# A decoder layer with expert lookup: where the first output projection keeps its tiles, and how a half-filled tile is picked

## The chip, the cores and the metric

The kernel runs on one core of a Trainium2 chip. A core has five engines that each work through a queue of their own in order: TensorE (PE, with its weight loads as PEld), VectorE (DVE), ScalarE (ACT), GpSimd (POOL) and SyncE (SP, which here only starts transfers). They wait for each other by semaphores. The metric is the device time of one execution in microseconds; a time is the median of several runs.

## The reference

One layer of a decoder over 1024 prompt tokens and 8 short sequences of 8 tokens (64 rows): two token mixers beside each other, an output projection, an expert mixer, and an embedding with a gate.

```python
def layer(h, p_l, pos, s_ret, s_wkv, s_shift, lp):
    xn = rmsnorm(h, norm_mix)
    proj = xn @ w_in
    ...                                   # retention in chunks of 128; RWKV-7 scan
    h = h + jnp.concatenate([o_ret, o_rw], axis=-1) @ w_out
    h = h + peer(rmsnorm(h, norm_ffn), peer_wq, peer_keys, peer_u, peer_v)
    gate = jax.nn.sigmoid((rmsnorm(h, ple_norm) @ ple_gate).astype(jnp.float32))
    h = h + (gate * (p_l @ ple_proj)).astype(h.dtype)

def peer(xn, wq, keys, u_tab, v_tab):     # per token, 8 heads, 2 half keys of 128
    q = (xb @ wq).reshape(PEER_BLOCK, PEER_HEADS, 2, PEER_DKEY // 2)
    s = jnp.einsum('phcd,hcnd->phcn', q, keys).astype(jnp.float32)
    sv, si = lax.top_k(s, PEER_TOPK)                        # 16 best of 128, for 16 (h, c)
    cand = sv[:, :, 0, :, None] + sv[:, :, 1, None, :]
    cv, ci = lax.top_k(cand.reshape(...), PEER_TOPK)        # 16 best pairs of each head
    e = ...                                                 # 128 expert numbers a token
    gsm = jax.nn.softmax(cv, axis=-1)
    hval = jnp.einsum('pd,phkd->phk', xb, u_tab[e])
    act = jax.nn.gelu(hval) * gsm
    return jnp.einsum('phk,phkd->pd', act, v_tab[e])
```

All matrices are float32; the output is all rows after a last norm, and the mixers' states.

## The kernel before

The 1088 rows are nine tiles of rows: tiles 0 to 7 hold 128 prompt tokens each, tile 8 the 64 sample rows. The work goes in stages.

*Input projections.* `group_a` runs three times, over tiles 0 and 1 (A0), 2 and 3 (A1), 4 to 8 (A2). It normalises and transposes the rows (`norm_T`, PSUM tile `ntr`), multiplies by `w_ret` (`a_ret`, PSUM tile `pret`, weights `wraw`, `wh`, `wl`) and by `w_rw` (`a_rw`, `prw`). Each float32 product is three matmuls of rounded halves (`mm3`, lines 336, 337 and 339). PSUM tiles come from banks with a tag: `a` has two buffers, `b` three, `d` one. A2 takes `pret` and `prw` from `b`; its `ntr` came from `a`.

*First tile.* While A1 runs, tile 0 goes through the mixers (`first_mix`, up to the tile `tail`) and then through the output projection, `c_rows`: transposes (`etr`), sixteen matmuls with blocks `cw` of `w_out` (`ewo`, line 625), the residual `ch`, the norm with rows `cgr`, and the store of the normalised row to memory (`xd`). `c_rows` took its tiles from a pool `co0` with a ring of six for blocks of 2 KB a partition. That pool lay behind A1's pools and was closed with them.

*Early experts.* `early` loads tile 0's row again (`exn`, line 1215), computes its query (`epq`), its top-k, and then its experts one by one: `gather` fetches for the j-th expert of 128 tokens a row of `u` each (an indirect DMA from POOL, `grow`, line 1161), which VectorE multiplies with the token (line 1175); then the same with `v` and a sum (line 1189). Tile 1 follows. Tiles 8, 2 and 3 are gathered in the same way later; tile 8 has its 64 rows laid twice, so that 128 partitions hold half of a token's experts each.

*Mixers.* `group_b` takes the other eight tiles through both mixers and `c_rows` (in a pool `co`, ring of four), with early's gathers in between.

*Query.* `c_query` goes over 16 pairs of head and half key: weights, `pq` for two groups of tiles, the scores `psc` for each tile, and for each tile a `pick` of five VectorE operations (16 best of 128). `topk` then combines them and makes the expert numbers (`eq`, `ef`). For tile 8 its numbers were copied by DMAs to the second half of the partitions.

*Dense experts.* Tiles 4 to 7 use all experts with a mask: `hidden`, `gates`, `dense_fused`, `dense_stored` (`ph`, `py`, `yT`), while the gathers of tiles 8, 2 and 3 go on beside them. `ple` ends the layer, tile by tile, tile 3 last: it adds tile 3's sum `gacc` (line 1447).

What decides the order on each engine: the code is written as generators that are stepped in turn (`interleave`, `behind`); a scheduler at build time then orders each engine's instructions by priority and its own estimate of durations. Pools stand on one stack on the right side of SBUF, and a tile that takes over the memory of a closed pool waits for the last use of what lay there.

## Time and profile before

| | us |
|---|---|
| median of 3 runs | 3610.72 (3601.78 to 3620.93) |
| profiled execution, its own time | 3621.93 |
| its span | 3620.2 |
| end of A1 on TensorE | about 262 |
| first `pret` of A2 | 307.73 |
| end of A2's projections on TensorE | about 573 |
| mixers end, last `hns` of `pY` | 1579.5 |
| query stage, first and last score matmul | 1637.3, 1809.5 |
| dense stage, first and last sum into `yT` | 2456.1, 3451.7 |

The profiled execution took 11 us more than the median, so sums are made against its own time and carried to the median afterwards. Rows of the timeline read: start, length, engine (with q: its queue of transfers and waits), line, operation, what it writes and reads, count, and in brackets the idle time before it and what ended that. The rows with two ends and many columns are stretches of the span.

### The profile page before, as it was taken

What the parts mean: (1) busy time and instruction counts of PE and PEld (TensorE: products, weight loads), DVE (VectorE), ACT (ScalarE), POOL (GpSimd) and SP (SyncE); (2) the same over time, 40 slices, a digit from 0 to 9 for tenths busy, and PEclk for the clock granted to TensorE, in tenths of its full rate; (3) what the DMA queues carried; (4) which work ended last, traced back from release to release, by engine and by line L of the source; (5) the groups of instructions that cost most, each with busy time, mean ns of one, the idle gap of its engine ahead of it and who ended that gap; (6) DMA issues with size and microseconds to landing.
All of it is one profiled execution on the core that took longest, in us unless ns stands there. A gap on an engine that the chain in (4) does not pass through costs nothing. (4 is left out here: it accounts for less than half of the span.)

```text
span 3620.2 us, 51709 instructions
## 1 busy us (share of the span) xinstructions
PE 3231.2 (89%) x17493; PEld 2670.2 (74%) x17493; DVE 2832.0 (78%) x5630; ACT 1227.0 (34%) x2263; POOL 2340.1 (65%) x2082
## 2 busy tenths in 40 slices
PE   7997996887868988879999999999999998899997
PEld 7886995664746766748877878778888887667775
DVE  4643688887797877869977899867777778788787
ACT  4332221111111111113234888853333333444322
POOL 5632677554345555635478777668888878888764
PEclk9998996657878777789999999999999999999999
DMA  7637699889857888897569889899999999999986
GB/s 266 192 121 233 202 333 318 278 285 315 294 184 280 312 288 279 305 324 238 163 202 313 326 313 338 309 327 340 340 343 345 341 335 369 372 377 367 324 293 217
DMA packets 416996, 1058.93 MB, mean 293 GB/s; under 512 B 45595, under 2 KB 141209, under 8 KB 412058
## 3 DMA queue, kind: packets, MB, share of 16 engines
q0 software_dynamic: 165888, 604.05, 46.9%
q1 hardware_dynamic: 198046, 364.18, 30.1%
q10 hardware_dynamic: 52796, 87.38, 6.5%
q8 instruction: 139, 2.28, 0.3%
q14 instruction: 127, 1.04, 0.1%
HBM read 968.09 MB, written 87.29 MB: 292 GB/s over the span
## 5 line engine op out<-in xcount | busy, mean ns | idle before, releaser
L1161 POOL DMA_INDIRECT grow<-in_pv,eid x576 | 565.1, 981 | 494.2 <-DVE gacc L1189 284.4
L1161 POOL DMA_INDIRECT grow<-in_pu,eid x576 | 564.3, 980 | 341.5 <-DVE grow L1175 200.9
L1189 DVE SCALAR_TENSOR_TENSOR gacc<-grow,ac,gacc 128x1024 f32<-128x1024 f32 x571 | 731.4, 1281 | 41.7 <-DMA grow<-in_pv,eid 35.8
L1175 DVE SCALAR_TENSOR_TENSOR grow<-grow,gacc 128x1024 f32<-128x1024 f32 x576 | 688.5, 1212 | 77.2 <-DMA grow<-in_pu,eid 72.4
L1351 PE MATMUL py<-ah,vh 128*128 128x512 f32 x1024 | 403.8, 395 | 27.0 <-ACT vh L307 26.9
L336 PE MATMUL ph<-cx,uh 128*128 128x512 f32 x1024 | 405.5, 396 | 5.0 <-ACT uh L307 5.0
L337 PE MATMUL ph<-cx,uh 128*128 128x512 f32 x1024 | 404.5, 395 | 0.0
L1352 PE MATMUL py<-al,vh 128*128 128x512 f32 x1024 | 402.0, 393 | 1.9 <-DVE al L309 1.7
L311 POOL TENSOR_TENSOR vl<-vraw,vh 128x512 fp32r<-128x512 f32 (+2 forms) x232 | 328.6, 1420 | 29.8 <-ACT vh L307 23.7
L311 POOL TENSOR_TENSOR ul<-uraw,uh 128x1024 fp32r<-128x1024 f32 x128 | 307.8, 2407 | 47.8 <-ACT uh L307 24.9
L1354 PE MATMUL py<-ah,vl 128*128 128x512 f32 x1024 | 277.6, 399 | 11.4 <-POOL vl L311 11.2
L339 PE MATMUL ph<-cx,ul 128*128 128x512 f32 x1024 | 262.8, 394 | 4.4 <-POOL ul L311 4.4
L307 ACT ACTIVATE vh<-vraw 128x512 fp32r<-128x512 f32 (+2 forms) x232 | 156.2, 675 | 284.6 <-DMA vraw<-in_pvd 87.6
L1351 PEld LDWEIGHTS py<-ah,vh 128*128 128x128 f32 x1024 | 193.7, 189 | 79.0 <-ACT vh L307 37.5
L1354 PEld LDWEIGHTS py<-ah,vl 128*128 128x128 f32 x1024 | 189.9, 188 | 65.5 <-POOL vl L311 23.1
L1358 DVE TENSOR_TENSOR yT<-yT,py 128x512 f32<-128x512 f32 x224 | 152.8, 684 | 100.0 <-PE py L1354 90.6
L336 PEld LDWEIGHTS ph<-cx,uh 128*128 128x128 f32 x1024 | 193.7, 189 | 46.2 <-ACT uh L307 6.5
L1352 PEld LDWEIGHTS py<-al,vh 128*128 128x128 f32 x1024 | 193.8, 189 | 43.4 <-DVE al L309 2.1
L337 PEld LDWEIGHTS ph<-cx,uh 128*128 128x128 f32 x1024 | 193.7, 189 | 38.9
L339 PEld LDWEIGHTS ph<-cx,ul 128*128 128x128 f32 x1024 | 189.9, 188 | 43.5 <-POOL ul L311 6.1
L307 ACT ACTIVATE uh<-uraw 128x1024 fp32r<-128x1024 f32 x128 | 135.4, 1057 | 150.0 <-DMA uraw<-in_puT 80.5
L311 POOL TENSOR_TENSOR wl<-wraw,wh 128x1024 fp32r<-128x1024 f32 x45 | 113.2, 2516 | 100.5 <-ACT wh L307 69.6
(411 smaller groups left out, 7169.3 us busy)
## 6 DMA issues: line engine op xcount, KB each, us to landing
uraw<-in_puT SPq DMA_DIRECT2D x128, 512.0 KB
vraw<-in_pvd SPq DMA_DIRECT2D x112, 320.0 KB
cw<-in_w_out SPq DMA_DIRECT2D x128, 256.0 KB
wd<-wst ACTq DMA_DIRECT2D x28, 1024.0 KB
wt<-wd SPq DMA_DIRECT2D x64, 448.0 KB
vraw<-in_pvd SPq DMA_DIRECT2D x112, 256.0 KB
wraw<-in_w_ret SPq DMA_DIRECT2D x48, 512.0 KB
wraw<-in_w_rw SPq DMA_DIRECT2D x42, 512.0 KB
```

What stands on the lines that cost most here:

```text
L307: nc.scalar.activation(hi, src, AF.Copy)
L311: nc.gpsimd.tensor_tensor(lo, src, hi.bitcast(F32), op=OP.subtract)
L336: mm(out, lh(k), rh(k), start=first and k == 0, stop=False)
L337: mm(out, *((ll(k), rh(k)) if right else (lh(k), rl(k))), start=False, stop=False)
L339: mm(out, *((lh(k), rl(k)) if right else (ll(k), rh(k))), start=False, stop=last and k == nk - 1)
L1161: nc.gpsimd.indirect_dma_start(out=g, out_offset=None, in_=src, in_offset=bass.IndirectOffsetOnAxis(ap=self.eid[t][:, j:j + 1], axis=0))
L1175: nc.vector.scalar_tensor_tensor(g[:, c], g[:, c], 1.0, x[:, c], op0=OP.mult, op1=OP.mult, accum_out=hv[:, i, j:j + 1])
L1189: nc.vector.scalar_tensor_tensor(y[:, c], g[:, c], ac[:, j:j + 1], y[:, c], op0=OP.mult, op1=OP.add)
L1351: nc.tensor.matmul(p, vh[:, b, :], ah, start=b == 0, stop=False)
L1352: nc.tensor.matmul(p, vh[:, b, :], al, start=False, stop=False)
L1354: nc.tensor.matmul(p, vl[:, b, :], ah, start=False, stop=b == nb - 1)
L1358: nc.vector.tensor_tensor(yT[:, d, :], yT[:, d, :], p, op=OP.add)
```

## The change

Three edits.

1. `co0` is gone. The pool `co` is opened before A0's pools, at the bottom of the right-hand stack, and closed after `early`'s; the first `c_rows` uses it with the ring of four that the later tiles use.
2. A2's `ntr` comes from bank `b` (three buffers) in place of `a`; A0 stays with `a`, A1 with `b`.
3. Tile 8 in `c_query`: the 16 pairs are taken in the order 0, 8, 1, 9, and so on. The scores of pair j go to partitions 0 to 63 of a PSUM tile `p8` (bank `d`), those of pair j + 8 to partitions 64 to 127; one copy and one `pick` of 128 partitions serve both. So tile 8 has 8 picks in place of 16, and in `topk` four heads on 128 partitions in place of eight on 64. The result lies as the gather wants it, and the four DMAs that copied halves are gone.

```diff
@@ group_a
-                self.norm_T(wp, r, n, gr, x[0], x[1], off[t], bank="b" if tiles == A1 else "a")
+                self.norm_T(wp, r, n, gr, x[0], x[1], off[t], bank="a" if tiles == A0 else "b")
@@ c_query
-        for hc in range(16):
+        for hc in [h + 8 * j for h in range(8) for j in range(2)]:
...
+                full = [t for t in tiles if t != 8]
...
+                if 8 in tiles:
+                    j = hc // 8
+                    if j == 0:
+                        p8 = self.ps("p8", "d")
+                    nc.tensor.matmul(p8[64 * j:64 * j + 64, :128], qT[:, off[8]:off[8] + 64], kT, start=True, stop=True)
+                    if j == 1:
+                        s8 = wp.tile([128, 128], F32, name="s8", bufs=2)
+                        nc.scalar.activation(s8, p8[:, :128], AF.Copy)
+                        self.pick(self.found[8], hc - 8, s8, 128)
                 p = self.ps("psc", "a")
-                for i, t in enumerate(tiles):
-                    nc.tensor.matmul(p[:SIZE[t], i * 128:i * 128 + 128], qT[:, off[t]:off[t] + SIZE[t]], kT, start=True, stop=True)
-                m = len([t for t in tiles if t == 8])
-                for t in tiles[:m]:
-                    nc.scalar.activation(s[:64, 0], p[:64, :128], AF.Copy)
...
+                for i, t in enumerate(full):
+                    nc.tensor.matmul(p[:, i * 128:i * 128 + 128], qT[:, off[t]:off[t] + 128], kT, start=True, stop=True)
@@ topk
-        n = SIZE[t]
+        n, H = (128, 4) if t == 8 else (SIZE[t], 8)
...
-        for h in range(8):
+        for h in range(H):
...
-        if t == 8:
-            ei = tp.tile([128, 128], I32, name="ei", tag="ex")
-            nc.vector.tensor_copy(ei[:n], ef[:n])
-            for k in range(2):
-                nc.scalar.dma_start(self.eid[t][64 * k:64 * k + 64], ei[:64, 64 * k:64 * k + 64])
-                nc.scalar.dma_start(self.gsm[t][64 * k:64 * k + 64], gsm[:64, 64 * k:64 * k + 64])
-        elif t not in G2:
+        if t not in G2:
             nc.vector.tensor_copy(self.eid[t][:n], ef[:n])
@@ build
+            co = self.co = sb("co", ec, side="right")
             pools = self.a_pool(e1, "1")
...
-            co0 = sb("co0", e1, side="right")
...
-                yield from self.c_rows(co0, E0[0], 6)
+                yield from self.c_rows(co, E0[0])
...
-            co = self.co = sb("co", ew, side="right")
...
+            ec.close()
```

How the built order moves. TensorE at the first output projection, before (`etr` are the transposes of tile 0's rows, `ewo` the projection, `ntr` and `pret` belong to A2):

```order
L608 MATMUL etr<-csta,tail 128x128 x4
L625 MATMUL ewo<-cw,coT 128x512 x16
L330 MATMUL ntr<-csta,njunk 128x128 x8
L336 MATMUL pret<-wh,x_3206 128x256
L330 MATMUL ntr<-csta,njunk 128x128 x4
```

The same place in the changed kernel:

```order
L608 MATMUL etr<-csta,tail 128x128 x4
L625 MATMUL ewo<-cw,coT 128x512 x5
L330 MATMUL ntr<-csta,njunk 128x128 x8
L625 MATMUL ewo<-cw,coT 128x512
L330 MATMUL ntr<-csta,njunk 128x128 x8
L625 MATMUL ewo<-cw,coT 128x512
L336 MATMUL pret<-wh,x_3202 128x256
```

Sixteen steps in one piece became seven with two tiles' transposes between them, and nine more spread over the first four tiles of A2.

SP's queue of transfers at that place, before (`ekT` are keys of the early query, `sr` and `ch` belong to tiles of the mixers, `exn` is tile 0's row for its query):

```order
L1230 DMA ekT<-in_keysT 128x128 x2
L437 DMA sr<-in_s_ret 64x512 x8
L598 DMA ch<-in_x 128x1024
L624 DMA cw<-in_w_out 128x512 x10
L637 DMA cgr<-in_rows 128x512 x2
L247 DMA row_norm_mix<-in_rows 128x1024
L379 DMA wraw<-in_w_ret 128x1024 x2
L361 DMA x<-in_x 128x1024 x2
L395 DMA rope<-in_rope 128x256
L1215 DMA exn<-xd_84 128x1024
```

And now:

```order
L1230 DMA ekT<-in_keysT 128x128 x2
L247 DMA row_norm_mix<-in_rows 128x1024
L379 DMA wraw<-in_w_ret 128x1024 x2
L361 DMA x<-in_x 128x1024
L624 DMA cw<-in_w_out 128x512
L361 DMA x<-in_x 128x1024
L395 DMA rope<-in_rope 128x256 x2
L624 DMA cw<-in_w_out 128x512
L395 DMA rope<-in_rope 128x256
L379 DMA wraw<-in_w_ret 128x1024
```

A2's loads moved ahead of the output weights `cw`, which are dealt out one by one among them, and `exn` stands 28 such rows behind `ekT` in place of 9.

POOL at tile 8's top-k, before (`ul` is a split for the dense stage; `eid_67` are tile 8's expert numbers):

```order
L1109 TENSOR_TENSOR eq<-eid,cf 64x800 x2
L311 TENSOR_TENSOR ul<-uraw,uh 128x1024
L1109 TENSOR_TENSOR eq<-eid,cf 64x800
L311 TENSOR_TENSOR ul<-uraw,uh 128x1024
L1109 TENSOR_TENSOR eq<-eid,cf 64x800 x2
L311 TENSOR_TENSOR ul<-uraw,uh 128x1024
L1109 TENSOR_TENSOR eq<-eid,cf 64x800
L311 TENSOR_TENSOR ul<-uraw,uh 128x1024
L1109 TENSOR_TENSOR eq<-eid,cf 64x800 x2
```

And now, up to the first gathers (lines are 7 or 8 higher in this part of the changed kernel):

```order
L1117 TENSOR_TENSOR eq<-eid,cf 128x800
L311 TENSOR_TENSOR ul<-uraw,uh 128x1024
L1117 TENSOR_TENSOR eq<-eid,cf 128x800
L311 TENSOR_TENSOR ul<-uraw,uh 128x1024
L1117 TENSOR_TENSOR eq<-eid,cf 128x800 x2
L311 TENSOR_TENSOR ul<-uraw,uh 128x1024
L1085 TENSOR_TENSOR sf<-sf,csta 128x256
L1161 DMA grow<-in_pu,eid_67 128x1024 x5
```

Eight steps became four, and before, the eight `sf` and `eid` steps of tile 4 stood between the last of them and the first gather.

Counted along the same order, the gathers (576 of `u` and 576 of `v` in all) stand so: ahead of the last step of A2's projections on POOL 68 before and 60 now; ahead of the mixers' last `hns` on VectorE 446 and 446; ahead of the first mask of the dense stage (line 1331) 667 and 677; behind the last sum into `yT` (line 1358) 63 and 54.

More of the change, by code (lines that the diff above doesn't have):

```diff
@@ L1033, in c_query @@
                 off, n = spans(tiles)
-                s = wp.tile([128, len(tiles), 128], F32, name=f"ss{tiles[0]}", bufs=SB)
+                full = [t for t in tiles if t != 8]
+                s = wp.tile([128, len(full), 128], F32, name=f"ss{full[0]}", bufs=SB)
                 p = self.ps("pq", "b")
                 self.mm3(p[:, :n], lambda k: wh[:, k, :], lambda k: wl[:, k, :], lambda k: x[0][:, k], lambda k: x[1][:, k], 8)
-                qT = wp.tile([128, n], F32, name=f"qT{tiles[0]}", bufs=1)
+                qT = wp.tile([128, n], F32, name=f"qT{full[0]}", bufs=1)
                 nc.scalar.activation(qT, p[:, :n], AF.Copy)
-                p = self.ps("psc", "a")
-                for i, t in enumerate(tiles):
-                    nc.tensor.matmul(p[:SIZE[t], i * 128:i * 128 + 128], qT[:, off[t]:off[t] + SIZE[t]], kT, start=True, stop=True)
-                m = len([t for t in tiles if t == 8])
-                for t in tiles[:m]:
-                    nc.scalar.activation(s[:64, 0], p[:64, :128], AF.Copy)
-                nc.scalar.activation(s[:, m:], p[:, m * 128:len(tiles) * 128].rearrange("p (t k) -> p t k", k=128), AF.Copy)
-                for i, t in enumerate(tiles):
-                    self.pick(self.found[t], hc, s[:, i], SIZE[t])
+                if 8 in tiles:
[7 more added lines that the diff above has]
+                        self.pick(self.found[8], hc - 8, s8, 128)
+                p = self.ps("psc", "a")
+                for i, t in enumerate(full):
+                    nc.tensor.matmul(p[:, i * 128:i * 128 + 128], qT[:, off[t]:off[t] + 128], kT, start=True, stop=True)
+                nc.scalar.activation(s, p[:, :len(full) * 128].rearrange("p (t k) -> p t k", k=128), AF.Copy)
+                for i, t in enumerate(full):
+                    self.pick(self.found[t], hc, s[:, i], 128)
             yield
@@ L1069, in topk @@
                 yield
-        sf = tp.tile([128, 8, 2, 16], F32, name="sf")
+        sf = tp.tile([128, 8, 2, 16], F32, name="sf")[:, :H]
         if t in G1 + G2:
@@ L1102, in topk @@
             yield
-        cf = tp.tile([128, 128], F32, name="cf", tag="cf" if ce else "sf")
+        cf = tp.tile([128, 128], F32, name="cf", tag="cf" if ce else "sf")[:, :16 * H]
         nc.scalar.activation(cf[:n], ci[:n].rearrange("p h k -> p (h k)"), AF.Copy, scale=STEP)
-        ef = tp.tile([128, 128], F32, name="ef", tag="ef" if ce else "ci")
-        for h in range(8):
+        ef = tp.tile([128, 128], F32, name="ef", tag="ef" if ce else "ci")[:, :16 * H]
+        for h in range(H):
             hs = slice(16 * h, 16 * h + 16)
@@ L1498, in build @@
             self.setup()
-            em, ee, eg, et, ew, ex, ep, e0, e1, e2 = (ExitStack() for _ in range(10))
+            em, ee, eg, et, ew, ex, ep, ec, e0, e1, e2 = (ExitStack() for _ in range(11))
             acc = self.acc = self.pool("psumg", space=PS, es=eg, reuse_waits="tile")
@@ L1540, in build @@
             parts = [G1, G2]
-            self.layout(cq, [(f"ss{g[0]}", [128, len(g), 128], F32, SB) for g in parts] +
-                        [(f"qT{g[0]}", [128, spans(g)[1]], F32, 1) for g in parts])
+            self.layout(cq, [(f"ss{[t for t in g if t != 8][0]}", [128, len([t for t in g if t != 8]), 128], F32, SB) for g in parts] +
+                        [(f"qT{[t for t in g if t != 8][0]}", [128, spans(g)[1]], F32, 1) for g in parts])
             cf = sb("cf8", ew, side="right")
@@ L1553, in build @@
                 fp = cf if t == 8 else tp
-                self.found[t] = (fp.tile([128, 16, 16], F32, name=f"sv{t}"), fp.tile([128, 16, 16], U32, name=f"si{t}"))
+                w = 8 if t == 8 else 16
+                self.found[t] = (fp.tile([128, w, 16], F32, name=f"sv{t}"), fp.tile([128, w, 16], U32, name=f"si{t}"))
             self.e12 = {}
```

27 lines of the change are left out of this document (13 added, 14 removed).

## The prediction

> **What bounds the kernel now.** I read the page first, then the stage table over the whole span, then ten-microsecond slices around the place where the diff cuts, then the rows of TensorE, SP and ScalarE there, and the end of the chain last.
>
> ```profile
> span 3620.2 us, 51709 instructions
> PE 3231.2 (89%) x17493; PEld 2670.2 (74%) x17493; DVE 2832.0 (78%) x5630; ACT 1227.0 (34%) x2263; POOL 2340.1 (65%) x2082
> ```
>
> ```profile
> 575.00:1000.00 425.00, 327.08 (x1863) 248.41 (x1864) 352.50 (x550) 59.96 (x136) 216.73 (x215) 0.68 0.87 299
> 1000.00:1580.00 580.00, 490.66 (x2797) 384.48 (x2795) 477.51 (x950) 100.56 (x198) 316.04 (x313) 0.79 0.80 276
> ...
> 1640.00:1800.00 160.00, 160.00 (x909) 139.07 (x908) 159.12 (x793) 47.59 (x88) 78.54 (x59) 1.00 0.60 198
> 1800.00:1880.00 80.00, 77.93 (x353) 63.91 (x352) 58.30 (x313) 31.28 (x44) 50.48 (x43) 1.00 0.51 161
> 1880.00:1960.00 80.00, 72.47 (x306) 57.95 (x307) 53.73 (x117) 20.21 (x28) 72.11 (x59) 0.98 0.94 332
> 1960.00:2390.00 430.00, 400.99 (x2192) 342.27 (x2191) 387.87 (x698) 365.17 (x780) 312.25 (x249) 0.98 0.88 320
> 2390.00:2960.00 570.00, 570.00 (x2499) 468.68 (x2498) 430.24 (x613) 176.67 (x264) 485.62 (x394) 1.00 0.96 338
> ...
> 3450.00:3620.00 170.00, 141.74 (x648) 110.71 (x648) 135.62 (x147) 42.98 (x78) 82.89 (x104) 0.95 0.74 252
> ```
>
> The columns are start, end, length, and then the busy time of PE, PEld, DVE, ACT and POOL, the clock, the DMA share and GB/s. The reader is to see two different halves. From 1640 us on TensorE is the bound: 160.00 of 160 us in the query stage, 570.00 of 570 in the first dense stretch. What VectorE saves there is worth only what TensorE's few idle microseconds give back. In the mixers (575 to 1580) neither engine is full: VectorE has 352.50 of 425 and 477.51 of 580, TensorE stands at a granted clock of 0.68 and 0.79, and the two wait for each other hop by hop, with gathers in between.
>
> The hole is earlier, between the second and the third group of projections:
>
> ```profile
> 260.00:270.00 10.00, 1.86 (x16) 1.66 (x15) 7.20 (x12) 0.90 (x2) 2.64 (x3) 0.79 0.40 116
> 270.00:280.00 10.00, 9.94 (x20) 4.67 (x21) 0.00 (x0) 0.60 (x1) 0.00 (x0) 0.69 0.58 187
> 280.00:290.00 10.00, 7.61 (x18) 2.93 (x16) 1.38 (x2) 1.15 (x2) 0.00 (x0) 0.99 0.79 258
> 290.00:300.00 10.00, 0.00 (x0) 0.00 (x0) 1.41 (x2) 1.04 (x2) 0.74 (x2) 0.50 0.77 270
> 300.00:310.00 10.00, 4.05 (x16) 3.40 (x17) 5.57 (x9) 4.63 (x9) 5.99 (x5) 0.50 0.81 296
> ```
>
> The same stretch by rows, TensorE first, then SP's queue, then ScalarE's queue:
>
> ```profile
> 270.06 1.11 PE L608 MATMUL etr<-csta,tail 128*128 128x128 f32 x4 [8.20 <-DVE tail L996]
> 270.96 16.65 PE L625 MATMUL ewo<-cw,coT 128*128 128x512 f32 x32
> 305.80 1.97 PE L330 MATMUL ntr<-csta,njunk 128*128 128x128 f32 x8 [18.19 <-DVE njunk L321]
> 307.73 0.58 PE L336 MATMUL pret<-wh,x 128*128 128x256 f32 x1
> ```
>
> ```profile
> 260.95 0.80 SPq L1230 DMA_DIRECT2D ekT<-in_keysT  x2
> ...
> 272.90 9.74 SPq L624 DMA_DIRECT2D cw<-in_w_out  x10
> ...
> 285.44 0.42 SPq L247 DMA_DIRECT2D row_norm_mix<-in_rows  x1
> ...
> 286.87 10.38 SPq L361 DMA_DIRECT2D x<-in_x  x2
> ...
> 302.06 0.33 SPq L1215 DMA_DIRECT2D exn<-xd  x1
> ```
>
> ```profile
> 298.57 0.34 ACTq L643 DMA_DIRECT2D xd<-ch  x1
> ```
>
> After tile 0's tail, TensorE does nothing but the output projection (270.96 to 287.6), then idles 18.19 us. The third group's first load (the norm row, 285.44) stands in SP's queue behind the last weight of that projection; its memory is the projection's own. From the end of the second group (about 262) to the third group's first projection at 307.73 are 46 us.
>
> **The change, part by part.**
>
> *The projection's buffers.* They now come from a pool that lies below both groups' pools, so SP sends the third group's norm row, two weight blocks and the first rows straight after the keys (260.95), ahead of all but four of the output weights. Then SP waits for the first of these matmuls (270.96) to free a slot of the ring of four, and only then sends the second rows, which TensorE's order wants before the first `pret`. In the profile the way from that second load (it ends its issue at 297.25) to `pret` (307.73) took 10.5 us; from 271 that gives 281. So the third group starts 27 us sooner. Bounds: 38 us (nothing but the loads to wait for, from about 262) and 0.
>
> What it costs: nine of the sixteen projection steps now stand among the third group's matmuls. Sixteen took 16.65 us at a clock of 0.69 to 0.99, so nine take 9 us at most. Here the clock rule is weighed. By the row, the clock fell to 0.50 in the empty slice. The Trainium skill, "TensorE: Matmul & The Clock Gate", Part 1, says that the array runs at half its clock after about 3.4 us of idleness and at full clock after as much work; the trace agrees (0.50, then 1.00 later). By that rule nine steps among busy neighbours cost about half, 5 us, an estimate from that page; the sum would be 4 us better. I keep 9.
>
> The end of the third group so comes 27 - 9 = 18 us sooner (about 557 instead of 575).
>
> *What is late next.* The same interleaving ends the projection later: the last step now stands behind four tiles' norms and some sixty projection matmuls, near 305 instead of 287.6. Tile 0's normalised row then goes to memory (298.57 before), comes back (302.06), its query is computed, and its gathers begin.
>
> ```profile
> 420.00:430.00 10.00, 0.77 (x1) 1.00 0.39 123
> ```
>
> ```profile
> 500.00:600.00 100.00, 48.92 (x47) 0.88 0.94 327
> ```
>
> ```profile
> POOL grow L1161 <- DVE gacc L1189: 122.8, 68, 8.6
> ```
>
> ```profile
> L1189 DVE SCALAR_TENSOR_TENSOR gacc<-grow,ac,gacc 128x1024 f32<-128x1024 f32 x571 | 731.4, 1281 | 41.7 <-DMA grow<-in_pv,eid 35.8
> L1175 DVE SCALAR_TENSOR_TENSOR grow<-grow,gacc 128x1024 f32<-128x1024 f32 x576 | 688.5, 1212 | 77.2 <-DMA grow<-in_pu,eid 72.4
> ```
>
> The first gather came at about 429 (the one in that slice). I expect it at 429 to 445, so the third group's head start is not matched by the gathers. The order says the same without a time: on POOL the third group's last step stood behind 68 gathers, now behind 60, while the last mixer step on VectorE stands behind as many as before (446). Eight gathers move into the mixers. Each costs VectorE 1.21 to 1.28 us, which is the floor (8 x 1.25 = 10 us), and at most the pace of 47 in 100 us, 2.1 us (17 us). POOL waits for VectorE there (122.8 us between 450 and 1000), so I am nearer the floor: 12 us. Left at the end of the mixers: 18 - 12 = 6 us; bounds: 27 won (nothing given back) and 10 lost (no head start, and the gathers' floor price paid).
>
> *The norm's bank.* Ten PSUM tiles of transposes (two for each of five tiles of rows) move from the two buffers shared with the early query to the three shared with `pret`. No row shows either sharing as a wait of size. Zero, within 3 us either way, counted in the bounds.
>
> *The half tile in pairs.* Eight picks of five VectorE operations go away, and in tile 8's top-k four heads of eight.
>
> ```profile
> L1057 DVE FIND_INDEX8 si<-sv,ss 128x8 uint32<-128x128 f32 (+1 forms) x112 | 30.0, 275 | 0.0
> ...
> L1056 DVE MAX8 sv<-ss 128x8 f32<-128x128 f32 (+1 forms) x112 | 26.2, 267 | 0.0
> ```
>
> ```profile
> 1836.89 1.53 POOL L1109 TENSOR_TENSOR eq<-eid,cf 64x800 f32<-64x800 f32 x1 [2.84 <-ACT cf L1104]
> ...
> 1862.28 1.53 POOL L1109 TENSOR_TENSOR eq<-eid,cf 64x800 f32<-64x800 f32 x1 [1.09 <-DVE ef L1111]
> ...
> 1872.20 0.96 POOL L1161 DMA_INDIRECT grow<-in_pu,eid  x1 [3.05 <-issue]
> ```
>
> ```profile
> 1866.31 1.13 ACTq L1132 DMA_DIRECT2D eid<-ei  x2
> ```
>
> Five operations of about 0.27 us, overlapping a little, are 1.2 us a pick: 8 x 1.2 = 10 us of VectorE. Of the eight `eq` steps (1836.89 to 1863.8, 27 us) half go: 13 us. The indices' detour through a DMA (1866.31 to the first gather, 1872.20) goes: 5 us. Tile 8's gathers so start some 25 us sooner against the query stage. On the path this is worth little at once, because TensorE is full there. Between 1800 and 2390 it idles 2.1 + 7.5 + 29.0 = 38.6 us; I take 4 of them back (0 to 15).
>
> *The end.* What the earlier gathers buy shows last:
>
> ```profile
> L1161 POOL DMA_INDIRECT grow<-in_pv,eid x23: 940/980/1398, 3541.2 to 3586.5; - x23
> ```
>
> ```profile
> 3595.29 1.22 DVE L1447 TENSOR_TENSOR ph<-ph,gacc 128x1024 f32<-128x1024 f32 x1
> ```
>
> ```profile
> PE ntr L330 <- DVE ph L1447: 10.9, 1, 10.9
> ```
>
> The last tile waits for the last gather, 10.9 us on TensorE. By the order, 63 gathers stood behind the last dense accumulation, now 54; nine of them at this stage's pace (23 in 45.3 us, 2.0 us each) are 18 us. The wait's 10.9 and a little of the stage's other gaps are all that TensorE can give: 12 us (0 to 18).
>
> The sum: 6 + 4 + 12 = 22 us. The profiled execution took 3621.93 us; it would be 3600. It lies 11 us above the median of 3610.72, so the median becomes 3589.
>
> **Rivals.**
>
> *The head start is kept (about 3561).* If the mixers are held by their own chain and not by VectorE's load, the eight gathers fall into its idle time (72 us of 425). For it: that idle time. Against: VectorE is at 83% there and in order. Then 27 - 5 + 10 + 18 = 50 us.
>
> *Only the tail gains (about 3600).* The twelve of the end are all, because gathers eat the whole head start: 3599. If the order's nine gathers are lost as well, nothing is left and the time is 3611; that is also the case in which the change does not do what it says, because the third group's tiles still wait for memory that the projection holds.
>
> *The gathers pace the mixers (about 3631, slower).* SP is one queue in order; nine output weights each wait for a matmul and hold the third group's loads, and the reverse. If the projection ends 32 us later (320), the first gather comes at 461, and if the mixers are paced by gathers, they end 32 us later; less the 12 of the end, 20 us are lost. It decides from a first gather about 30 us late. For it: POOL's rate of 47 in 100 us with DMA at 0.94. Against: POOL waits for VectorE there, not the reverse. The Trainium skill, "DMA: Bandwidth & Descriptors", "Issuing engines are not separate DMA queues", says that all DMAs share the same 16 engines and interleave, which speaks for this rival; the slices at 0.77 to 0.81 leave a fifth free.
>
> **How the numbers follow.** The forecast has a chance of 0.47, of which 0.33 lies beyond 0.5%, which is 18 us and about what a measurement of this kernel can tell from no change; the kept head start 0.17; the tail alone or nothing 0.26; the slower one 0.10. Faster 0.50, same 0.40, slower 0.10. The range reaches from just below the kept head start, 3558, to 3616, and leaves out the slower case and the far end of the first rival. The forecast's own range is 3575 to 3605.
>
> **What would show it.** Right: first `pret` near 281; the third group's end near 557; first gather 429 to 445; the mixers' last step a few us earlier; first gather of tile 8 less than 50 us behind the last query matmul; no 10 us wait before the last tile's transposes. Wrong: a `pret` start after 300 (another wait on memory took over), a first gather after 455, or a last gather that again ends the kernel.

## The result, and the profile after

| | us |
|---|---|
| median before, beside the change | 3606.48 (3601.78 to 3620.93) |
| median after | 3575.01 (3558.17 to 3581.87) |
| ratio | 0.9904, 95% interval 0.9877 to 0.9931 |

The change makes the kernel faster: the medians lie 31 us apart, and the ratio of the two sets of runs says 35 us (0.96%). A second comparison, *all_again* below, gave 0.9874 (0.9853 to 0.9895), which is 46 us. The forecast was 3589, which is 22 us less than 3610.72, with a range of 3558 to 3616. The profiled execution of the changed kernel took 3581.87 us, 40 less than the profiled one of before:

```profile
span 3580.1 us, 51586 instructions
PE 3248.4 (91%) x17493; PEld 2679.9 (75%) x17493; DVE 2807.8 (78%) x5530; ACT 1223.3 (34%) x2255; POOL 2328.6 (65%) x2078
```

The hole between the second and third group, in the same ten-microsecond slices as before (start, end, length, busy time of PE, PEld, DVE, ACT and POOL, clock, DMA share, GB/s):

```profile
260.00:270.00 10.00, 1.81 (x14) 1.61 (x13) 7.37 (x16) 0.92 (x2) 2.64 (x3) 0.72 0.70 236
270.00:280.00 10.00, 9.12 (x23) 3.82 (x21) 4.06 (x3) 5.64 (x9) 4.69 (x5) 0.77 0.66 213
280.00:290.00 10.00, 7.47 (x41) 5.02 (x40) 5.46 (x9) 4.55 (x7) 3.62 (x5) 1.00 1.02 392
290.00:300.00 10.00, 10.00 (x59) 7.31 (x58) 7.23 (x9) 3.43 (x6) 3.58 (x7) 1.00 0.62 203
300.00:310.00 10.00, 9.70 (x80) 8.97 (x80) 4.92 (x11) 3.58 (x6) 2.50 (x6) 1.00 0.67 217
```

From 290 on TensorE is full at a clock of 1.00, where it stood empty at 0.50. SP's queue and TensorE's rows say how: the third group's norm row, weights and first rows go out straight behind the keys (260.28), the second rows at 272.57, and its first `pret` starts at 282.65 instead of 307.73, between matmuls of the output projection.

```profile
260.28 0.80 SPq L1230 DMA_DIRECT2D ekT<-in_keysT  x2
261.13 0.42 SPq L247 DMA_DIRECT2D row_norm_mix<-in_rows  x1
261.66 0.85 SPq L379 DMA_DIRECT2D wraw<-in_w_ret  x2
262.55 0.43 SPq L361 DMA_DIRECT2D x<-in_x  x1
272.20 0.33 SPq L624 DMA_DIRECT2D cw<-in_w_out  x1
272.57 0.43 SPq L361 DMA_DIRECT2D x<-in_x  x1
```

```profile
270.26 6.79 PE L625 MATMUL ewo<-cw,coT 128*128 128x512 f32 x10
277.61 1.09 PE L330 MATMUL ntr<-csta,njunk 128*128 128x128 f32 x8 [0.57 <-DVE njunk L321]
...
282.65 0.68 PE L336 MATMUL pret<-wh,x 128*128 128x256 f32 x1
```

Further landmarks, before and then after: the last `prw` (572.9, 538.8; the row gives shortest, median and longest duration in ns, then first and last start in us), the gathers of `u` and of `v` (first 429.2 and 423.3, last 3586.5 and 3541.9), and the head norms of the mixers (last 1579.5 and 1557.9).

```profile
L337 PE MATMUL prw<-x,wh x448: 276/290/682, 68.4 to 572.9; 128*128 128x256 f32 x75, 128*128 128x288 f32 x75
L337 PE MATMUL prw<-x,wh x448: 275/290/682, 68.4 to 538.8; 128*128 128x256 f32 x75, 128*128 128x288 f32 x75
L1161 POOL DMA_INDIRECT grow<-in_pu,eid x576: 932/947/1946, 429.2 to 3254.8; - x192
L1161 POOL DMA_INDIRECT grow<-in_pu,eid x576: 932/946/1802, 423.3 to 3197.4; - x192
L1161 POOL DMA_INDIRECT grow<-in_pv,eid x576: 932/946/2597, 661.1 to 3541.9; - x192
L420 DVE TENSOR_REDUCE hns<-pY x8: 662/683/692, 764.2 to 1579.5; 128x8 f32<-128x512 f32 x7, 64x8 f32<-64x512 f32 x1
L420 DVE TENSOR_REDUCE hns<-pY x8: 630/688/692, 717.8 to 1557.9; 128x8 f32<-128x512 f32 x7, 64x8 f32<-64x512 f32 x1
```

The mixers' stretch from the third group's last step to the last head norm, gathers alone (start, end, length, POOL's busy time and count, clock, DMA share, GB/s), before and after: eight gathers more, 11.7 us longer. How far a single pair can be trusted here is said with the experiments.

```profile
579.80:1579.50 999.70, 384.67 (x381) 0.74 0.83 286
546.50:1557.90 1011.40, 387.79 (x389) 0.73 0.83 287
```

At the half tile, its numbers are converted in place at 1817.53 and its first gather goes out at 1819.67, 37 us behind the last score matmul (1783.0; before 63, 1809.5 to 1872.20). At the end TensorE's longest wait was 10.9 us for the last gather; now no wait for it is left, and no single wait of the last tiles' transposes is above 3.3 (lines 1452 and 1458 are other steps than the sum of line 1447).

```profile
L1051 PE MATMUL psc<-keysT,qT x192: 271/275/582, 1610.6 to 1783.0; 128*128 128x128 f32 x192
```

```profile
1817.53 1.37 DVE L1135 CAST eid<-ef 128x64 int32<-128x64 f32 x1
```

```profile
1819.67 0.97 POOL L1161 DMA_INDIRECT grow<-in_pu,eid  x1
```

```profile
PE ntr L330 <- DVE ph L1452: 5.9, 2, 3.3
PE ntr L330 <- DVE ph L1458: 2.6, 2, 2.0
```

### The profile page after: what moved, and what is told of

Same layout as the page of the kernel before. It is cut to its first block, busy times and chain, and to the rows that moved or that the text cites. A ratio compares the mean times of both kernels' runs of the same rounds, so it can differ in the third digit from the quotient of the medians.

```text
span 3580.1 us, 51586 instructions
## 1 busy us (share of the span) xinstructions
PE 3248.4 (91%) x17493; PEld 2679.9 (75%) x17493; DVE 2807.8 (78%) x5530; ACT 1223.3 (34%) x2255; POOL 2328.6 (65%) x2078
## 5 line engine op out<-in xcount | busy, mean ns | idle before, releaser
L339 PEld LDWEIGHTS ph<-cx,ul 128*128 128x128 f32 x1024 | 191.2, 189 | 42.2 <-POOL ul L311 4.2
L311 POOL TENSOR_TENSOR wl<-wraw,wh 128x1024 fp32r<-128x1024 f32 x45 | 113.4, 2519 | 88.3 <-ACT wh L307 64.8
```

The source lines that it names most:

```text
L311: nc.gpsimd.tensor_tensor(lo, src, hi.bitcast(F32), op=OP.subtract)
L339: mm(out, *((lh(k), rl(k)) if right else (ll(k), rh(k))), start=False, stop=last and k == nk - 1)
```

## The experiments

All are made from the changed kernel by undoing edits or adding one thing. Ratios are to the kernel before on the same chip (medians there 3622 to 3627 us, so times are compared as ratios). The landmarks come from one profile each; two profiles of the changed kernel differ by 15 us at the first head norm of the mixers' `pY` (717.8 and 732.8), by 6 at the last (1557.9 and 1563.5), and by 2 at the end, so a landmark in the mixers tells no less than that. *e3_half_tile* and the kernel before differ by more: up to the last head norm their orders are the same, and still that norm lies 14 us apart (1565.4 and 1579.5). A difference of 15 us at the mixers' end between two single profiles is therefore no finding by itself; what is read from there is read from groups of profiles, or from the times.

| kernel | edits | ratio (95%) | first `pret` | last `prw` | last head norm | last query matmul | end |
|---|---|---|---|---|---|---|---|
| before | | | 307.7 | 572.9 | 1579.5 | 1807.4 | 3620.2 |
| e1_buffers | 1 | 0.9960 (0.9939 to 0.9982) | 286.9 | 569.6 | 1583.5 | 1805.6 | 3616.2 |
| e2_bank | 2 | 0.9944 (0.9922 to 0.9966) | 306.4 | 553.8 | 1565.7 | 1787.9 | 3604.2 |
| e3_half_tile | 3 | 0.9971 (0.9948 to 0.9995) | 305.2 | 571.9 | 1565.4 | 1791.3 | 3590.2 |
| e12_buffers_bank | 1, 2 | 0.9963 (0.9943 to 0.9984) | 284.0 | 542.1 | 1560.5 | 1783.1 | 3598.8 |
| e13_buffers_half | 1, 3 | 0.9955 (0.9936 to 0.9974) | 286.3 | 567.5 | 1574.1 | 1796.0 | 3593.9 |
| e23_bank_half | 2, 3 | 0.9905 (0.9880 to 0.9930) | 309.6 | 557.7 | 1568.5 | 1791.0 | 3585.5 |
| all_again | 1, 2, 3 | 0.9874 (0.9853 to 0.9895) | 281.2 | 541.4 | 1563.5 | 1785.7 | 3578.2 |
| late_three | 1, part of 2 | 0.9946 (0.9928 to 0.9964) | 288.9 | 548.3 | 1565.0 | 1785.4 | 3603.7 |

(Last query matmul: start of the last `pq` of line 339; end: the span.)

### Each edit alone and in pairs

*e1_buffers*: edit 1 alone.

```diff
-                self.norm_T(..., bank="a" if tiles == A0 else "b")
+                self.norm_T(..., bank="b" if tiles == A1 else "a")
...                                        # and c_query, topk as before
```

> Edit 1 alone (the first projection in the later tiles' pool, with a ring of four); the norm's bank and the half tile as before. In the order of this kernel 67 gathers stand on POOL ahead of the third group's last step (68 before, 60 after all three edits), and 379 gathers lie on VectorE between the third group's last step and the last mixer's head norm (384 before, 392 after all three). Theory K (the head start is kept: the third group is bound by TensorE, and the mixers give back only the price of the gathers that are moved, 11.8 us for 8 between the two traces, 1.5 us each): first pret near 283; first pret to last prw 256 us as after all three edits, so the last prw near 539; the stretch from the third group's last step to the last head norm 5 x 1.5 = 7 us shorter than before, 992; the mixers end 35 to 40 us sooner than before; time near 3575. Theory F (the forecast: nine steps of the output projection add 9 us to the third group): first pret to last prw 274, last prw near 557; without moved gathers the mixers end 18 us sooner; time near 3588. Rival B (the bank of the norms is what let TensorE close its gaps, and the buffers alone do not): first pret to last prw 265 as before or longer, last prw near 548; time near 3582.

The start came as the buffers promise (286.9), but the third group then took 282.7 us from first `pret` to last `prw`, 17.5 more than before, so that its end is 3 us sooner and the mixers' end is 4 us later, which is scatter. Theories K and F both fall; B named the place ("265 as before or longer"), though its last `prw` of 548 came 22 us too early. The rows of TensorE show why:

```profile
298.68 1.13 PE L625 MATMUL ewo<-cw,coT 128*128 128x512 f32 x2 [0.64 <-DMA cw<-in_w_out]
...
313.28 1.94 PE L1221 MATMUL etr<-csta,exn 128*128 128x128 f32 x8 [11.58 <-DMA exn<-xd]
316.18 1.65 PE L1239 MATMUL epq<-exT,ewq 128*128 128x128 f32 x6 [0.96 <-ACT exT L1222]
317.62 0.42 PE L330 MATMUL ntr<-csta,njunk 128*128 128x128 f32 x1
```

The third group's transposes (`ntr`), the projection (`ewo`) and the early query (`etr`, `epq`) take the two buffers of bank `a` in turn. So the `ntr` of tiles 6, 7 and 8 stand behind the early query's transposes, and those wait 11.58 us for tile 0's row to come back from memory, with TensorE in order behind them. In this kernel the wait on memory was not removed, it was moved.

*e12_buffers_bank*: edits 1 and 2 (half tile as before).

> Edits 1 and 2 (buffers and the norms' bank), the half tile as before. 60 gathers stand on POOL ahead of the third group's last step and 392 between it and the last head norm on VectorE, as with all three edits. Theory K: first pret to last prw 256, mixers' stretch 1011 us (999 before), first matmul after the mixers 27 us sooner than before; the end without the half tile's gain: time 3606 - 27 = 3579, with the last tile waiting about 10 us for the last gather again. Theory F: mixers' end 6 us sooner, 3600. Rival T (the tail gains from the earlier mixers, not from the half tile): no wait of 10 us before the last tile's transposes, and 3566 to 3570.

With the bank the last `ntr` (304.53) stands ahead of the early query, which comes when its row is back (`etr` at 320.09 without a wait on memory), and the third group takes 258.1 us. K is right on the third group (256) and close at the last query matmul (24 us sooner, 27 expected), but the time says 13 us (6 to 21) where K expected 27; F's 6 us for the whole is at the edge of that. The last tile waits 9.5 us for the last gather again, so T falls.

```profile
304.53 0.71 PE L330 MATMUL ntr<-csta,njunk 64*128 64x64 f32 x8
...
320.09 1.04 PE L1221 MATMUL etr<-csta,exn 128*128 128x128 f32 x8
```

*late_three*: edit 1, and the bank of three only for tiles 6, 7 and 8.

```diff
-... bank="b" if tiles == A1 else "a")
+... bank="b" if tiles == A1 or t > 5 else "a")
```

> Edit 1, and of the third group's five tiles only the last three (6, 7 and 8) have their norms in the bank of three; half tile as before. With edit 1 alone the transposes of tiles 4 and 5 stood ahead of the early query's on TensorE and those of 6, 7 and 8 behind them. Theory W: these three are the whole of it; no wait of TensorE for tile 0's row (11.6 us with edit 1 alone), first pret to last prw 256 to 262 us (282.7 with edit 1 alone, 258.1 with edits 1 and 2), time as with edits 1 and 2, 19 us less than before. Theory S (every transposed tile in the shared bank costs its share): two fifths of the 24.6 us stay, third group 268 us; time 8 to 12 us less than before.

Theory W holds here: with the three tiles alone in the other bank no wait for tile 0's row is left, the third group takes 259.4 us, and the ratio is that of e12_buffers_bank or better.

*e2_bank*: edit 2 alone.

> Edit 2 alone: the third group's norms in the bank of three, the projection's buffers and the half tile as before. Theory W (the bank is worth something only where the third group's rows come before tile 0's row is back from memory, because in the shared bank of two their transposes turn behind the early query's; with buffers and old bank TensorE waited 11.6 us for that row and the third group's projections took 283 us, with buffers and new bank 258): here memory holds the first pret at about 307 anyway, so the third group takes 262 to 266 us (265 before) and the time is within 5 us of before. Theory S (sharing a bank of two costs the third group something by itself, whatever its start): the third group is 9 or more us shorter, 256 or less, and the time 8 to 12 us less than before. The forecast: 0, 3 either way.

Theory W falls, and with it the forecast's zero: the bank alone shortens the third group to 247.4 us, 17.7 less than before, and the kernel by 0.56%. Theory S had the direction and was too small (256 or less, 8 to 12 us). Even where memory holds the start at 306, the bank of before had cost. Slices of before and then of e2_bank (columns as above):

```profile
320.00:340.00 20.00, 16.70 (x125) 15.88 (x126) 12.77 (x41) 6.23 (x15) 2.33 (x6) 0.91 0.55 173
440.00:460.00 20.00, 15.47 (x99) 14.32 (x99) 11.59 (x21) 3.76 (x7) 11.33 (x11) 0.83 0.98 366
460.00:480.00 20.00, 15.57 (x113) 15.37 (x112) 17.24 (x31) 3.98 (x8) 11.00 (x10) 0.83 0.93 322
```

```profile
320.00:340.00 20.00, 19.23 (x156) 18.06 (x155) 11.87 (x48) 6.64 (x16) 4.31 (x8) 1.00 0.52 161
440.00:460.00 20.00, 17.15 (x139) 16.48 (x138) 16.69 (x33) 4.31 (x8) 13.19 (x13) 1.00 1.03 406
460.00:480.00 20.00, 18.53 (x143) 18.07 (x143) 17.05 (x33) 5.56 (x11) 13.26 (x13) 1.00 0.98 351
```

TensorE got through 125 matmuls in 320 to 340 where it now does 156, and its clock fell to 0.83 at 440 to 480 where it now holds 1.00. There was no one long wait to see, only short ones (none above 4.4 us) and a lower clock behind them. From 308 to 573 us before, and from 306 to 554 us in e2_bank, TensorE ran 1952 and 1943 matmuls; it stood idle for 14.8 and 6.9 us, and was busy for 250.2 and 241.1 us.

The 17.7 us arise in two places, and only one of them is where transposes of the rows turn in a ring with the early query. The `pret` matmuls alone, before and then e2_bank, each from the first to the 301st and from the 501st to the last (start, end, length, busy time of PE, PEld, DVE and ACT, clock, DMA share, GB/s):

```profile
307.73:389.40 81.67, 44.04 (x301) 38.09 (x302) 8.40 (x22) 0.00 (x0) 0.96 0.64 204
413.10:483.50 70.40, 61.36 (x462) 59.50 (x460) 3.99 (x10) 7.24 (x19) 0.90 0.83 293
```

```profile
306.36:380.90 74.54, 39.83 (x300) 36.57 (x301) 8.26 (x22) 0.00 (x0) 1.00 0.65 214
404.60:464.20 59.60, 56.25 (x462) 54.89 (x460) 3.38 (x9) 7.13 (x19) 1.00 0.86 319
```

The first part, with the transposes and the early query in it, is 7 us shorter; some 2 of these are only moved ahead of the first `pret`, where e2_bank does more of the transposes. The second part is 11 us shorter, and there TensorE runs nothing but `pret`: the early query and the norms are done, and the first gathers begin in it (429.2 and 417.3). Its waits there are put down to `retd` on VectorE (4.4 us before, 1.2 in e2_bank) and to nothing that the profile shows (4.5 and 2.1). All four profiles without edit 2 take 69 to 71 us for this part, and all nine with it (one of them late_three, with a part of it) 59 to 64, so the gain belongs to the edit, but by what way moving the transposes, which are done by then, comes to shorten it was not found.

*e3_half_tile*: edit 3 alone.

> Edit 3 alone (the half tile picked in pairs); buffers and bank as before. Up to the end of the mixers the order is that of before (446 gathers ahead of the last head norm), so nothing should move there. In the order 1092 of the 1152 gathers stand ahead of the last dense accumulation (1089 before, 1098 after all three edits). Forecast: first one-hot step (oh) 18 to 25 us sooner against the last query matmul (151 us before), 4 us kept by the first yT; the tail gains three gathers of 2 us, 6; together 10 us: 3596. Theory Z (TensorE is full from the query on and the tail is bound by its own work): 3602 to 3606, within 0.2%. Theory D (VectorE bounds the query and what follows, so its saved 10 us and POOL's saved 13 us count in full): 3583 or less.

From the last query matmul to the end it took 1798.9 us, 14 less than before (1812.8), near the forecast's 4 + 12 = 16 for the whole change. By the times it is 0.29% (10 us, as forecast for this edit alone), 0.05 to 0.52%: theory D's 0.64% falls, theory Z's 0.2% is not excluded by the times alone. The first one-hot step came 30 us sooner against the last query matmul (123.6 for 153.5). Where the gain shows was not as forecast: 18 us by the first write of `yT`, none at the end, where the last tile still waits 6.6 us for the last gather. Of the 16 us that this profile is ahead at the last query matmul, 14 are there at the last head norm, ahead of anything that the edit touches; they are the scatter of the mixers.

*e13_buffers_half*: edits 1 and 3.

> Edits 1 and 3, the third group's norms in the bank of before: all three edits without the second. 67 gathers on POOL ahead of the third group's last step, 379 on VectorE between it and the last head norm (60 and 392 with all three), 1099 of 1152 ahead of the last dense accumulation (1098). If the bank is worth nothing on the path (forecast: 0, 3 us either way): within 3 us of the time with all three edits, 3572 to 3578. Theory K, with 1.5 us for each gather moved: mixers' stretch 992 instead of 1011, so if the third group is as short as with the bank, the mixers end 15 to 19 us sooner than with all three: 3556 to 3560, faster than the changed kernel. Rival B (the bank closes TensorE's gaps in the third group): third group 9 us longer, so 3565 to 3569, or 3575 to 3580 where the moved gathers are worth nothing.

0.9955, where all three give 0.9874 or 0.9904: beside the buffers the bank is worth about 0.5 to 0.8%, not zero, and the forecast's 3 us either way is outside that. K's mixers of 992 us were not seen (1001.6). The third group took 281.2 us, with a wait of 12.1 for tile 0's row: 25 us longer than after, where rival B expected 9.

*all_again* and *e23_bank_half*: the changed kernel once more, and edits 2 and 3 without the new buffers.

> The changed kernel itself, beside its parts. Edits 1 and 2 alone gave 19.5 us, edit 3 alone 14.1 us, edits 1 and 3 without the bank 18.2 us, edit 1 alone 15.9 us (each within about 8). If the pairs add up (buffers and bank in the front, half tile in the rear, no shared term): 34 us less than before, ratio 0.990 to 0.991. If they overlap (both pay for the same wait at the end): 20 to 24 us, ratio 0.993 to 0.9945.

> Edits 2 and 3 (the norms' bank and the half tile), without the projection's new buffers. In the order 67 gathers stand on POOL ahead of the third group's last step (60 with all three edits), 382 on VectorE between it and the last head norm (392), 1090 of 1152 ahead of the last dense accumulation (1098). If the edits add: bank alone 19.3 us, half tile alone 14.1 us, together 33 us less than before, ratio 0.9908, and the buffers are the rest of the 45 us. Theory M (the bank makes the front's gain, and the buffers' earlier start is eaten by the gathers that it leaves for the mixers): last query matmul within 5 us of the place that it has with all three edits, near 1787; the whole within 8 us of all three edits, ratio 0.9874 to 0.990. Rival K (the buffers' start is what is kept; bank and half tile are small): 15 us less than before, ratio 0.996.

The changed kernel came out faster than either of its expectations (0.990 to 0.991, and 0.993 to 0.9945). By the ratios, one edit and the other two together make 24 us (e12 and e3), 37 (e2 and e13) and 49 (e1 and e23); all three edits give 46 here and 35 in the first comparison. So front and rear add within the intervals for two of the pairs; the first falls short of the second comparison (0.66% against 1.26%) by more than the intervals allow, and why stays open. Inside the front the edits do not add: buffers and bank apart give 0.40 and 0.56%, together 0.37%. Bank and half tile alone give 0.9905, which is where they were expected if they add (0.9908), and carry most of the whole. What the buffers add to the bank is not shown by the times: 0.3% less time than e23_bank_half in one comparison, none in the other, and 0.2% more from e2_bank to e12_buffers_bank, all with intervals that overlap. By place they show a little: the last head norm lies at 1565.7 and 1568.5 in the two profiles with the bank alone, and at 1557.9 to 1565.0 in the six with both. Both kernels reach the last `yT` at 3415 us; what is left between them is the end, where e23_bank_half waits again for the last gather:

```profile
PE ntr L330 <- DVE ph L1447: 9.4, 1, 9.4
```

Theory M is nearly met, with the last query matmul at 1791.0 (5 to 10 us behind all three) and a ratio of 0.9905 where it had 0.9874 to 0.990. K falls.

### What a gather in the mixers costs

*skip32*: all three edits; 32 of tile 0's gathers left out.

```diff
+        if t == E0[0]:
+            nc.gpsimd.memset(hv[:, 0, 64:96], 0.0)
         for j in range(n):
+            if t == E0[0] and 64 <= j < 96:
+                yield j
+                continue
             g = fetch(I['pu'], j)
```

> All three edits, but 32 of tile 0's first 128 gathers and the VectorE steps on them (rows 64 to 95) are left out; those fall into the mixers. Theory G (in the mixers each gather costs the path its VectorE time or a little more: the forecast's 12 us for eight): 32 x 1.21 = 39 to 32 x 1.5 = 48 us less in the stretch from the third group's last step to the last head norm (1011 us), 963 to 972. Theory N (gathers ride in VectorE's idle time, and the 11 us that the mixers gave back come from elsewhere): 1000 or more. Between 972 and 1000: part of the price. In the time, the same less what the end gives back.

```profile
548.30:1511.70 963.40, 347.80 (x345) 0.75 0.81 278
549.00:1563.50 1014.50, 388.46 (x389) 0.73 0.83 287
```

The stretch from the third group's last step to the last head norm, in skip32 and then in all_again: 51 us less for 44 gathers less (the 32, and twelve that slid behind the mixers), 1.2 us each, about VectorE's duration for one (1.21). Theory G is met and N falls: the path pays for gathers there. Whether it pays for VectorE's step or for the transfer and POOL's issue with it, this run does not tell, since it leaves all three out. The twelve profiles with all gathers agree in size: from the last `prw` to the last head norm the six with 377 to 384 gathers in between took 992 to 1013 us, and the six with 392 took 1016 to 1026, 14 us more in the mean. In time 31 of the 51 us are left (3548.06 and 3579.32), 0.9793 (0.9761 to 0.9825); most of the rest goes behind the last query matmul, which has 1808.2 us to the end for 1792.5.

### What the half tile gives

*picks16*: all three edits, and each of the eight picks made twice.

```diff
+                        s9 = wp.tile([128, 128], F32, name="s9", bufs=2)
+                        nc.scalar.activation(s9, p8[:, :128], AF.Copy)
+                        self.pick(self.spare8, hc - 8, s9, 128)
```

> All three edits, with VectorE's saving given back: the eight picks of the half tile are made twice, the second time on a copy, into tiles that nothing reads (40 operations, 10 us of VectorE by their rows, and eight more ScalarE copies). In the order 1091 gathers stand ahead of the last dense accumulation (1098 without the extra picks). Theory P (TensorE is full in the query stage and VectorE's load there is free): from the first to the last query matmul 182 us as before, time within 3 us of all three edits. Theory D (VectorE sets the pace there): 8 to 10 us longer in the query stage or right behind it. Theory O (the end pays for each gather that stands behind the last dense accumulation, 2 us): seven more of them, 10 to 14 us longer, with a wait of 5 to 11 us for the last gather in front of the last tile's transposes.

*half_late*: all three edits, four `eq` steps of tile 8 repeated, and its numbers copied by two DMAs.

```diff
+        for h in range(4 if t == 8 else 0):
+            ...                            # the eq and ef steps of head h again
+            for k in range(2):
+                nc.scalar.dma_start(self.eid[t][64 * k:64 * k + 64], ei[64 * k:64 * k + 64])
```

> All three edits, with POOL's saving and the detour given back for tile 8: four of its eq steps are repeated and its indices go through a copying DMA, as before the change; VectorE's saving in the picks is kept. 1089 gathers ahead of the last dense accumulation. Theory E (what edit 3 gives comes from tile 8's gathers starting earlier): first one-hot step 16 to 20 us later against the last query matmul (135 us with all three edits, 153 before), and 13 to 20 us of time lost, the whole of edit 3. Theory D (it comes from VectorE's 10 us): 0 to 5 us lost. Theory O (only the number of gathers behind the last dense accumulation counts): 15 to 18 us lost as well, but at the end of the kernel, with the wait for the last gather back, not in front of the first one-hot step.

picks16: 0.9912 (0.9883 to 0.9942); half_late: 0.9924 (0.9897 to 0.9952); all three: 0.9874. From the last query matmul to the end: 1792.5 us (all_again; 1799.1 in the first profile), picks16 1803.9, half_late 1813.1, and 1812.8 before. So half_late loses the whole of edit 3 although VectorE keeps its saving in the picks (the repeated steps give 4 us of work back to it), and picks16 about half of it, although the query stage itself is no longer (from its first to its last `pq` 181 us, 183 in all_again). First one-hot steps of all_again, picks16 and half_late, beside last query matmuls at 1785.7, 1784.6 and 1786.2:

```profile
L1295 DVE TENSOR_TENSOR oh<-csta,pit x128: 1162/1214/1222, 1921.0 to 2341.1; 128x1024 f32<-128x1024 f32 x128
L1298 DVE TENSOR_TENSOR oh<-csta,pit x128: 1168/1215/1225, 1918.9 to 2337.1; 128x1024 f32<-128x1024 f32 x128
L1306 DVE TENSOR_TENSOR oh<-csta,pit x128: 1200/1217/1234, 1933.7 to 2349.3; 128x1024 f32<-128x1024 f32 x128
```

half_late is 12 us late there (E expected 16 to 20). In both the wait before the last tile's transposes is back, 7.6 us in picks16 and, in half_late:

```profile
PE ntr L330 <- DVE ph L1458: 9.1, 1, 9.1
```

Theory D falls for the query stage and what follows it: from the last query matmul to the first sum into `yT` picks16 takes 631.8 us, all_again 636.5. Both kernels start tile 8's gathers later, though, half_late by design and picks16 presumably because its longer line of picks holds back tile 8's top-k (46.7 us behind the last query matmul for 38.6). Over all profiles the place of that first gather goes with the time to the end, and the count of gathers left behind the last sum into `yT` does not (us behind the start of the last `pq` of line 339; gathers started behind the last sum):

| kernels | first gather of tile 8 | end | gathers left |
|---|---|---|---|
| five without edit 3 | 64.8 to 67.4 | 1810.6 to 1818.2 | 57 to 59 |
| half_late | 57.1 | 1813.2 | 59 |
| skip32 | 53.4 | 1808.2 | 56 |
| picks16 | 46.7 | 1804.0 | 57 |
| e23_bank_half, e3_half_tile | 42.2, 35.8 | 1794.5, 1798.9 | 58, 56 |
| e13_buffers_half, after, all_again | 43.3, 38.6, 38.6 | 1797.9, 1799.1, 1792.5 | 49, 50, 50 |

With 56 to 59 gathers left the end lies anywhere from 1794 to 1818, nearly in the order of the first gather; with 49 or 50 left it is hardly sooner than with 56 or 58. So theory E carries what edit 3 gives. O's wait at the end came back where it said, and the stretch behind the last sum is a few us longer with it (162.6 to 165.2 us with 49 or 50 left, 163.9 to 177.8 with more), but that is not where the whole is decided. picks16 and half_late also add work of their own, so that the early start is the only term is not shown.

## Why the prediction was right or wrong, point by point

The time lay inside the range, 14 us under the forecast and at the lower end of its own range (3575 to 3605). The saving was forecast as 22 us and came out as 31 to 46. Of the signs, a `pret` start near 281, tile 8's first gather within 50 us of the last query matmul (38.6) and no 10 us wait before the last transposes came true; the third group's end (538.8 for 557) and the first gather (423.3 for 429 to 445) did not.

*The start of the third group* (281, 27 us sooner): 282.65, 25 sooner. Right, through the loads named.

*Nine projection steps cost 9 us.* Right: their eighteen matmuls take 8.0 and 8.1 us in the two profiles of the changed kernel, one every 0.43 us, and with the bank in place the buffers lengthen the third group from 247.4 to 258.1 and from 248.1 to 260.2 (256.1 in the first profile), 8 to 12 us. The Trainium skill, "TensorE: Matmul & The Clock Gate", Part 1, has the array at half its clock after idleness; the trace agrees, with one matmul of the projection every 0.85 us at first and every 0.43 us from the sixth or seventh on, in both kernels. The prediction's 5 us by that rule came from halving the whole row of before, but only the first six or seven of its 32 matmuls were slow, up to about 276 us; the rest ran at a clock of 1.00.

*The norm's bank: zero, within 3.* This is the step that failed. It is worth 17.7 us of the third group alone (e2_bank), and 24.6 together with the buffers (282.7 to 258.1). The reason given was that no row of before shows the sharing as a wait of size. That was true and not enough. With the earlier start the sharing became one long wait (11.58 us in e1_buffers) that the trace of before could not hold. Without the earlier start the bank still gave 17.7 us, in short waits and a lower clock; 7 of these lie beside the shared ring, and for the other 11 the way is open. Hence the third group ended 34 us sooner, not 18, and with the buffers alone it ended 3 us sooner.

*What is late next.* The first gather was to come at 429 to 445; it came at 423.3. The row did go to memory later (loaded back at 312.53 for 302.06), but the query behind it ran faster. The eight gathers that move into the mixers were right in number (381 to 389) and about right in price: 12 us forecast, 1.2 us each by skip32, 14 us between the two groups of six profiles. The 11.7 us of the single pair lie within the scatter. But they were put down to the projection's later end; the order of the kernels apart shows 67 gathers ahead of the third group's last step with buffers alone (68 before) and 60 only with the bank as well, which lets the group end sooner. Left at the end of the mixers: 6 forecast, 21.6 and 16.0 at the last head norm against the one profile of before, but only 7.5 and 1.9 against e3_half_tile, whose order up to there is that of before. In the mean of the six profiles with buffers and bank against these two it is 10 us. The third group's end was 16 us off, but how much of that reached the mixers' end, single profiles cannot tell.

*The half tile and the end* (4 + 12): 14 to 20 us from the last query matmul to the end; over all kernels, 1792.5 to 1799.1 us with edit 3 and 1810.6 to 1818.2 without. Right in sum, and in part by luck, because the places were not. TensorE's idle time from 1800 to 2390 was 38.6 us; in the stretch 27 us earlier it is 32.2 and 28.8 (said 4 less). The end itself gave 3 to 6 us of the 12 (from the last `yT`, 168.5 before, 165.2 and 162.6 after), and the rest lay in between. That nine gathers pass the last dense accumulation is so (60 to 51 behind it); that this count makes the gain is not: tile 8's earlier start does, as the table above shows.

*The rivals.* The kept head start came near the place of the last query matmul (26 and 22 us sooner, where it had 27 - 5 = 22) and, with 31 to 46 of its 50 us, nearer to the time than the forecast in the second comparison; but for another reason: its own condition, that the gathers ride free, falls with skip32, and the buffers alone win nothing at that place. The tail alone falls, since bank and buffers without the half tile win time too (0.9963, 0.9943 to 0.9984). The slower one falls at its first condition: the gathers began sooner, not 30 us later.

Open: whether the buffers give anything in the time once the bank is there, why the buffers alone show 0.40% in the times where their one profile shows 4 us, how the bank shortens the `pret` matmuls that stand behind all transposes, and where in the dense stage the half tile's lead turns into time, since it shows by the first `yT` in some kernels and at the end in others.

## What to carry to other kernels

Before an edit is priced at nothing because the profile shows no wait on what it separates, ask what that resource would hold up if the other edits work: two producers that turn in one ring of buffers are tied in order, and here the one that came early waited 11.58 us for the other's trip to memory. An earlier start is worth only what the next thing in the engine's order lets through, so follow the order behind it and not only the start. In the stretch where VectorE was 83% busy, each gather moved into it cost 1.2 us of the path, its full duration on VectorE. And a place where one profile is 14 us ahead of another may be scatter: a second kernel with the same order up to there tells.

## What the runs showed that was not expected

The third group of before had no wait above 4.4 us on TensorE and still hid 17.7 us, the difference that e2_bank shows. The same 320 matmuls, of before and then of e2_bank (busy time and mean ns of one, then idle time just before them and what ended it):

```profile
L336 PE MATMUL pret<-wh,x 128*128 128x256 f32 (+1 forms) x320 | 83.4, 294 | 6.8 <-DVE retd L412 4.4 <-issue 1.6 <-ACT x L307 0.7
```

```profile
L336 PE MATMUL pret<-wh,x 128*128 128x256 f32 (+1 forms) x320 | 79.2, 285 | 3.0 <-issue 1.6 <-DVE retd L412 1.2
```

The idle pieces are paid twice, once as time and once as a granted clock of 0.83 to 0.91 in the slices that hold them. Right behind a few of them sixteen matmuls of the early query took 3.64 us before, and the next sixteen 1.95, though no gap in the ten us ahead of them was above 1.6 us:

```profile
321.09 1.07 PE L330 MATMUL ntr<-csta,njunk 128*128 128x128 f32 x8 [1.58 <-DVE njunk L321]
...
323.98 3.64 PE L1239 MATMUL epq<-exT,ewq 128*128 128x128 f32 x16 [1.18 <-DVE x L309]
...
328.05 1.95 PE L1239 MATMUL epq<-exT,ewq 128*128 128x128 f32 x16
```
